# Residual rows of a projection loaded ahead, and its turns moved to the end of the next block

## The chip, the cores and the metric

One core of a Trainium2 chip runs the whole program. The metric is device time in microseconds (us) of one execution, the median of three runs. Profiles show one execution each; times in a profile count from the start of its span. The engines are PE (TensorE: matrix products), PEld (its weight loads), DVE (VectorE), ACT (ScalarE), POOL (GpSimd) and SP (SyncE, which issues the transfers).

## What is computed

The kernel is one layer of a decoder for 512 prompt rows and 32 sample rows (8 sequences of 4), width 1024. Three parts follow each other, each between two RMS norms and added to the residual:

```python
x = x + rms_norm(mix @ w_out, g_mix_post)
x = x + rms_norm(mem_attend(rms_norm(x, g_mem_pre), mk, mv, w_mq, w_mo), g_mem_post)
f, conv_new = conv_ffn(rms_norm(x, g_ffn_pre), conv_buf, w_up, w_dw, b_dw, w_down)
x = x + rms_norm(f, g_ffn_post)
```

The first is a mixer (mLSTM heads and differential attention), the second attends to 256 memory tokens and ends in the output projection `w_mo`, the third is a gated MLP of width 2752 with a causal convolution of three rows. The change lies at the end of the second: `o @ w_mo`, its norm, the sum with the residual, and the turn of the new rows for the products with `w_up`.

## The kernel before, in words

**Blocks.** The 544 rows are five blocks: 0 to 3 are prompt rows of 128, block 4 the 32 sample rows. Rows with the model width in the free dimension are what norms and sums need; products with `w_up` need them turned (width in the partitions). The turned rows are `fT`, in four tiles (a high and a low part for each half of the width, since every product of 32-bit numbers is made as three products of rounded parts: high x high, high x low, low x high).

**The projection.** `proj_add` (L1067) builds two passes over the five blocks, one for each half (512 columns) of `w_mo`. Pass 1 (`ev0`) leaves each block's first half, times the gain, in `y0`, and its sum of squares. Pass 2 (`second`, L1125) is the block-major branch of `gemmA` (L391 to L404): blocks in the order 4, 0, 1, 2, 3, and in each block eight steps k of three products (L387, L388, L389; for block 4 the sample's products at L367). Ahead of a block, `before(b)` (L1088) takes a tile `xb` from the pool N and issues the load of the block's residual rows from DRAM (L1091). After a block, `ev1` (L1093) does on ACT the square sum (L1076), on DVE the multiplication by the gain (L1100) and the sum of the square sums (L1101), on POOL the reciprocal root (`rstd`, L293 and L294), on DVE two operations `STT` (L1106: y times the root plus the residual rows, into `xb`), and on SP the store of the new rows (L1107). Then `rows_of` (L1112) puts the block on the list `pend` and takes on ACT the sum of squares of the new rows into a tile `hN` of the same pool N (L299), which becomes `rsd` (L1118).

**The turns.** `norm_turn` (L311) turns a block on `pend`: two times four transposes on PE (L318) into a PSUM tile `tp`, one multiplication by the next gain on DVE (L320, `ht`), a cast on ACT (L142) and a subtraction on POOL (L143), which write high and low part of `fT`. `mid` (L1121) is called at step `MIDK` = 4 of each block of pass 2 and turns one block if more than `LP` = 1 are pending. So block 4 is turned in the middle of block 1, block 0 in block 2, block 1 in block 3, and blocks 2 and 3 are still pending at the end.

**What follows.** `gemmB` with `half_first` (L433) makes the first four column tiles of `w_up`: first the columns 0 to 255 (blocks 0 and 1) of all four (L439, 128x256), then the columns 256 to 543 (blocks 2, 3 and 4; 128x288). After the first and the third tile (`POS` = (0, 2), L1612) a pending block is turned. The norm of the rows is applied afterwards: `spread` (L1529) makes `rsb`, the roots of all rows spread over the partitions, with a product for each block (L1533). The other tiles of `w_up` and the products with `w_down` go on to the end (L451, L1658 to L1660).

**Weights.** A list of weight tiles is loaded ahead into 6 staging tiles (`wst`; L227 for `w_mo`, L247 for `w_up`) and split on ACT and DVE (L142, L143) into 4 slots (`wslot`). The sample's products read the staging tile itself, so it stays in use until they are done.

**Pools.** N has 5 tiles of 1032 columns (`xb`, `hN`, and before them the queries and the conv rows `cr`); S has 11 large tiles (8.5 KB in each partition: `oT`, `fT`, the conv table `cvT`, keys and values of the memory, later `yp` and `act`). All loads are issued by SP, in one queue.

**Order.** A planner of the language's library sets the order of every engine's instructions from a simulated time line, with the written order as priority; waits are made by it too.

Of the kernel before, what the change touches and what calls it, by code (L numbers as in the profile page):

```python
# [7 lines left out]
F32 = mybir.dt.float32  # L8
# [7 lines left out]
P = 128  # L16
DM = 1024
# [56 lines left out]
def kernel(ctx: ExitStack, tc: tile.TileContext, I, O):  # L74
# [7 lines left out]
    MIDK, LR, LP, POS = 4, 0, 1, (0, 2)  # L82
# [15 lines left out]
    def S(shape, dt, name):  # L98
        return sp.tile(list(shape), dt, name=name, tag="S")

    def N(name, w=1024):
        return npool.tile([P, 1032], F32, name=name, tag="N")[:, :w]

    def T2(shape, name, dt=F32):
        return t2p.tile(list(shape), dt, name=name, tag="T2")

    def Z(name):
        return zp.tile([P, 512], F32, name=name, tag="Z")
# [4 lines left out]
    def mmp(name="mm"):  # L113
        return psm.tile([P, 512], F32, name=name, tag="mm")
# [20 lines left out]
    dma = nc.sync.dma_start  # L135
# [9 lines left out]
    def rows(b):  # L145
        return (b * P, P) if b < 4 else (SEQ, NS)
# [58 lines left out]
    def stage():  # L205
        return stg.tile([P, 1024], F32, name="wst", tag="st")
# [84 lines left out]
    def rstd(ss, n, w, dim, name="rs"):  # L291
        r = small(w, name)
        nc.gpsimd.tensor_scalar(out=r[:n], in0=ss, scalar1=1.0 / dim, scalar2=EPS, op0=MUL, op1=ADD)  # L293
        GTT(out=r[:n], in0=r[:n], in1=mhalf[:n, :w], op=ALU.pow)  # L294
        return r[:n]

    def sumsq(x, n, junk, name="ssq"):
        ss = small(1, name)
        ACT(out=junk, in_=x, func=AF.Square, accum_out=ss[:n])  # L299
        return ss[:n]  # L300
# [29 lines left out]
    class Fill:  # L330
# [8 lines left out]
        def run(self, amount=1e9):  # L339
            while amount > 0 and self.q:  # L340
                try:
                    amount -= next(self.q[0])
                except StopIteration:
                    self.q.pop(0)
# [15 lines left out]
    def sample_mm(ps, xs, w, start, stop):  # L360


        for kk, x in enumerate(xs):
            n = x.shape[0]
            for e in range(2):
                g = NS * (2 * kk + e)
                mm(ps[g:g + NS, :256], lhsT=x, rhs=w[:n, kk, 256 * e:256 * e + 256], start=start, stop=stop)  # L367

    def sample_sum(ps, dst):
        for e in range(2):  # L370
            c = slice(256 * e, 256 * e + 256)
            nc.scalar.copy(out=dst[:, c], in_=ps[NS * e:NS * e + NS, :256])
            VTT(out=dst[:, c], in0=ps[64 + NS * e:64 + NS * e + NS, :256], in1=dst[:, c], op=ADD)

    def gemmA(xt, nk, blocks, evac, block_major=False, before=None, mid=None):


        ps = {}

        def one(b, k, s):  # L380
            if b == 4:
                if k % 2 == 0:
                    sample_mm(ps[b], [xt.sam(k), xt.sam(k + 1)], s[1], k == 0, k == nk - 2)
                return
            s, kk = s[0], k % 2
            c0, n = rows(b)
            mm(ps[b], lhsT=xt.hi(k, c0, c0 + n), rhs=s[:, 0, kk, :], start=(k == 0), stop=False)  # L387
            mm(ps[b], lhsT=xt.hi(k, c0, c0 + n), rhs=s[:, 1, kk, :], start=False, stop=False)  # L388
            mm(ps[b], lhsT=xt.lo(k, c0, c0 + n), rhs=s[:, 0, kk, :], start=False, stop=(k == nk - 1))  # L389

        if block_major:  # L391
            slots = [W.get() for _ in range((nk + 1) // 2)]
            for b in blocks:
                if before:
                    before(b)
                ps[b] = mmp()
                for k in range(nk):
                    if k == MIDK and mid:
                        mid()
                    one(b, k, slots[k // 2])  # L400
                    if b == blocks[-1] and k % 2 == 1:
                        W.free()
                evac(b, ps[b])
                yield 5.1  # L404
        else:
            for b in blocks:
                ps[b] = mmp()
            behind = []
            for k in range(nk):
                if k % 2 == 0:  # L410
                    s = W.get()
                    if 4 in blocks:
                        behind.append((k, s))
                for b in blocks:
                    if b < 4:
                        one(b, k, s)
                if k % 2 == 1:
                    W.free()
                yield sum(0.64 for b in blocks if b < 4)
            for b in blocks:  # L420
                if b < 4:
                    evac(b, ps[b])
            if behind:
                for k, s in behind:
                    one(4, k, s)
                evac(4, ps[4])
                yield 4 * 0.53
            yield 0
# [199 lines left out]
    for c0, c1 in HALF:  # L628
# [5 lines left out]
        t = T2([64, n], "gt")  # L634
# [250 lines left out]
    for g in range(2):  # L885
        for h in range(0, H, 2):
            t = stage().rearrange("p (j b e) -> p j b e", j=2, b=4)
# [174 lines left out]
    def gbc(name):  # L1062
        g = cst.tile([P, 1028], F32, name="gb", tag="gb")
        dma(out=g[:, :DM], in_=I[name][0].partition_broadcast(P))
        return g[:, :DM]

    def proj_add(xt, gname, src, gname2, dst, order=None, scale=None):  # L1067

        g = gbc(gname)
        y0, s0, xb, pend, ready, target = {}, {}, {}, [], [], []  # L1070

        def ssq(b, y, nm):
            n = rows(b)[1]
            ss = sm.tile([P, 1], F32, name=nm, tag=nm, bufs=6)
            j = Z("sqj")
            ACT(out=j[:n], in_=y, func=AF.Square, accum_out=ss[:n])  # L1076
            return ss[:n]

        def ev0(b, ps):
            n = rows(b)[1]  # L1080
            z = y0[b] = T2([P, 512], "y0")[:n]
            if b == 4:
                sample_sum(ps, z)
                ps = z
            s0[b] = ssq(b, ps, "ssy0")
            VTT(out=z, in0=ps, in1=g[:n, :512], op=MUL)

        def before(b):  # L1088
            n = rows(b)[1]
            xb[b] = N("xb")[:n]  # L1090
            dma(out=xb[b], in_=src(b))  # L1091

        def ev1(b, ps):  # L1093
            c0, n = rows(b)
            z = T2([P, 512], "y1")[:n]
            if b == 4:
                sample_sum(ps, z)
                ps = z
            ss = ssq(b, ps, "ssy1")
            VTT(out=z, in0=ps, in1=g[:n, 512:], op=MUL)  # L1100
            VTT(out=ss, in0=s0[b], in1=ss, op=ADD)  # L1101
            rs = rstd(ss, n, 1, DM)
            x = xb[b]
            for i, z in enumerate((y0[b], z)):
                c = slice(512 * i, 512 * i + 512)
                STT(out=x[:, c], in0=z, scalar=rs, in1=x[:, c], op0=MUL, op1=ADD)  # L1106
            dma(out=dst[c0:c0 + n, :], in_=x)  # L1107
            ready.append((x, n, c0))
            while len(ready) > LR:
                rows_of(*ready.pop(0))  # L1110

        def rows_of(x, n, c0):  # L1112
            if scale is None:
                pend.append((norm_rows(x, n, ACTROWS), n, gname2, target[0], c0, POOLQ))
                return
            pend.append((x, n, gname2, target[0], c0, POOLQ))
            rs = sm.tile([P, 1], F32, name="rsd", tag="rsd", bufs=5)
            VCP(out=rs[:n], in_=rstd(sumsq(x, n, N("hN")[:n]), n, 1, DM))  # L1118
            scale[1].append((rs[:n], c0, n))

        def mid():  # L1121
            if len(pend) > LP:
                norm_turn(*pend.pop(0))

        def second(xt2):  # L1125
            target.append(xt2)
            run(gemmA(xt, 8, [4, 0, 1, 2, 3], ev1, block_major=True, before=before, mid=mid))
            while ready:
                rows_of(*ready.pop(0))
            while len(pend) > 2:  # L1130
                norm_turn(*pend.pop(0))
            return pend
        return gemmA(xt, 8, order or allb, ev0, block_major=order is not None), second
# [157 lines left out]
    pend = second(hqT)  # L1291
# [138 lines left out]
    for b in range(4):  # L1430
        t = mk_scores(b)
    with tc.issue_after(t):
        for j in range(8, 16):
            t = mk_turn(j)
# [7 lines left out]
    with tc.issue_after(t):  # L1442
        for b in range(4, NB):
            t = mk_scores(b)
# [81 lines left out]
    rsb = cst.tile([P, ROWS], F32, name="rsb")  # L1526
    rss = []

    def spread(i):  # L1529
        while rss and (i or len(rss) > 2):  # L1530
# [3 lines left out]
            VCP(out=rsb[:, c0:c0 + n], in_=ps[:, :n])  # L1534

    proj, second = proj_add(oT, "g_mem_post", lambda b: xd[0][rows(b)[0]:rows(b)[0] + rows(b)[1], :], "g_ffn_pre", xd[1],
                            scale=(rsb, rss))
    run(proj)
    pend = second(fT)

# [100 lines left out]
    for gi, js in enumerate(groups):  # L1641
# [6 lines left out]
        nk = len(js)  # L1648
# [41 lines left out]
        if not last:  # L1690
            behind = []
            for n0 in (0, 512):
                ps = [mmp() for _ in range(4)]
                for i in range(nk):
# [3 lines left out]
                    for b in range(4):  # L1698
                        t = one(b, ps[b], i, s)
# [124 lines left out]
```

## Time and profile before

| | us |
|---|---|
| median of 3 runs (lowest, highest) | 970.07 (969.19, 971.19) |
| the profiled execution's own time | 968.01 |
| its span, first to last instruction | 966.2 |
| PE busy in the span | 940.1 (97%) |
| DVE, ACT, POOL busy | 598.6, 388.0, 202.6 |
| mean granted clock | 0.989 of 2.4 GHz |

The span is what the engines took; 1.8 us lie around it. A busy PE is not a PE at its peak, since matrix products overlap each other; what counts is where it waits and which clock it is granted. The projection's pass 2 and the start of `w_up` lie at 520 to 583 us of the span.

### The profile page before, as it was taken

Reading aid. Unit: us, or ns where it says so; the run is one execution under the profiler, and the core shown is the slowest. Engines: PE = TensorE matmul, PEld = TensorE weight load, DVE = VectorE, ACT = ScalarE, POOL = GpSimd, SP = SyncE. Lnnn points to the kernel's source line nnn. Section 1 sums busy time; section 2 is a strip of 40 time slices with the busy share of each in tenths; the row PEclk is TensorE's granted clock in tenths of the full one; section 3 lists DMA queues with packets and bytes.
Section 4 is the critical chain, followed back from the end, with each engine's and each line's share of the span. In section 5 each row is a group of like instructions: output and inputs, shape, how many; then the busy total and the mean of one; then the engine's idle time right before and its main releaser. Section 6 shows DMA issues by size and latency. Waiting matters only on the chain.

```text
span 966.2 us, 17070 instructions
## 1 busy us (share of the span) xinstructions
PE 940.1 (97%) x6615; PEld 813.3 (84%) x6615; DVE 598.6 (62%) x1127; ACT 388.0 (40%) x746; POOL 202.6 (21%) x397
## 2 busy tenths in 40 slices
PE   8999999999999999999999799999999999999994
PEld 5999787779866788998767699989988997997983
DVE  6835145555786367625554759827758675675677
ACT  6744134343686367534533524332212222222232
POOL 6610000016332124200000544301110110110114
PEclk9999999999999999999999999999999999999997
DMA  9950024344835359846734844063053303503213
GB/s 303 299 160 1 1 88 134 88 126 133 256 100 173 133 180 322 258 144 209 287 133 128 229 138 128 4 174 89 5 142 79 120 25 91 150 25 90 86 48 114
DMA packets 120529, 130.27 MB, mean 135 GB/s; under 512 B 8551, under 2 KB 85960, under 8 KB 120448
## 3 DMA queue, kind: packets, MB, share of 16 engines
q1 hardware_dynamic: 114264, 125.69, 41.9%
q10 hardware_dynamic: 6184, 3.48, 1.2%
q8 instruction: 52, 0.85, 0.4%
q14 instruction: 29, 0.24, 0.1%
HBM read 112.22 MB, written 16.93 MB: 134 GB/s over the span
## 4 chain that ended last, share of the span: by engine, by line
PE 86%; DVE 4%; DMA 4%; ACT 2%; POOL 2%; issue 1%; SPq 0%; DVEq 0%; POOLq 0%; ACTq 0%
PE mm L451 32%; PE mm L439 8%; PE mm L387 6%; PE mm L389 6%; PE mm L388 6%; PE mm L1660 4%; PE mm L1659 4%; PE mm L1658 4%; PE mm L367 2%; PE tpk L1388 1%; PE sda L1183 1%; DMA xb<-in_x_prompt_dram 1%; DMA wst<-in_w_mo_dram 1%; PE sca L1339 1%; DVE wslot L143 1%
## 5 line engine op out<-in xcount | busy, mean ns | idle before, releaser
L451 PEld LDWEIGHTS mm<-fT,wslot 128*128 128x128 f32 x1872 | 234.3, 188 | 2.1 <-issue 1.2
L451 PE MATMUL mm<-fT,wslot 128*128 128x256 f32 (+1 forms) x1872 | 236.0, 288 | 0.0
L142 ACT CAST wslot<-wst 128x1024 fp32r<-128x1024 f32 x125 | 131.1, 1051 | 254.7 <-PE mm L451 76.0
L143 DVE TENSOR_TENSOR wslot<-wst,wslot 128x1024 fp32r<-128x1024 f32 x125 | 155.7, 1249 | 90.9 <-ACT wslot L142 90.9
L1659 PE MATMUL mm<-wslot,act 128*128 128x512 f32 x176 | 69.6, 396 | 0.0
L1660 PE MATMUL mm<-wslot,act 128*128 128x512 f32 x176 | 68.9, 397 | 0.0
L1658 PE MATMUL mm<-wslot,act 128*128 128x512 f32 x176 | 68.7, 392 | 0.0
L1565 POOL COPY cvo<-u 128x2 f32<-128x2 f32 x43 | 15.2, 354 | 201.2 <-DVE u L1563 191.2
L387 PE MATMUL mm<-wslot,hT 128*128 128x512 f32 x128 | 52.2, 408 | 0.0
L388 PE MATMUL mm<-wslot,hT 128*128 128x512 f32 x128 | 51.3, 401 | 0.0
L389 PE MATMUL mm<-wslot,hT 128*128 128x512 f32 x128 | 51.3, 402 | 0.0
L1560 DVE TENSOR_TENSOR u<-mm,rsb 128x256 f32<-128x256 f32 x43 | 18.2, 424 | 52.9 <-PE mm L451 50.9
L451 PE MATMUL mm<-hT,wslot 128*128 128x256 f32 (+1 forms) x384 | 51.0, 289 | 0.0
L451 PEld LDWEIGHTS mm<-hT,wslot 128*128 128x128 f32 x384 | 49.2, 188 | 0.8 <-issue 0.4
L1658 PEld LDWEIGHTS mm<-wslot,act 128*128 128x128 f32 x176 | 33.6, 191 | 8.6 <-issue 0.8
L1659 PEld LDWEIGHTS mm<-wslot,act 128*128 128x128 f32 x176 | 33.1, 188 | 7.2
L1660 PEld LDWEIGHTS mm<-wslot,act 128*128 128x128 f32 x176 | 33.1, 188 | 7.2
L1577 ACT ACTIVATE c<-c 128x560 f32<-128x560 f32 x21 | 14.1, 672 | 54.9 <-DVE c L1571 51.6
L1571 DVE SCALAR_TENSOR_TENSOR c<-u,cvT,c 128x560 f32<-128x560 f32 x43 | 34.2, 796 | 0.8
L1570 DVE SCALAR_TENSOR_TENSOR c<-u,cvT,c 128x560 f32<-128x560 f32 x43 | 34.1, 792 | 0.1
L439 PE MATMUL mm<-fT,wslot 128*128 128x256 f32 (+1 forms) x192 | 27.2, 303 | 2.6 <-POOL fT L143 2.4
L1671 DVE TENSOR_TENSOR yp<-mm,yp 128x512 f32<-128x512 f32 x40 | 27.1, 687 | 3.9 <-PE mm L1660 3.8
(469 smaller groups left out, 1868.3 us busy)
## 6 DMA issues: line engine op xcount, KB each, us to landing
wst<-in_w_up_dram SPq DMA_DIRECT2D x42, 512.0 KB
wst<-in_w_in_dram SPq DMA_DIRECT2D x28, 512.0 KB
wst<-in_w_down_dram SPq DMA_DIRECT2D x20, 512.0 KB
wst<-in_cache_mem_k_dram SPq DMA_DIRECT2D x16, 512.0 KB
wst<-in_w_mk_dram SPq DMA_DIRECT2D x8, 512.0 KB
xb<-in_x_prompt_dram SPq DMA_DIRECT2D x8, 512.0 KB
wst<-in_cache_dk_dram SPq DMA_DIRECT2D x16, 256.0 KB
wst<-in_cache_dv_dram SPq DMA_DIRECT2D x16, 256.0 KB
```

Source lines behind the costliest of these rows:

```text
L142: nc.scalar.copy(out=hi, in_=src)
L143: (eng or nc.vector).tensor_tensor(out=lo, in0=src, in1=f32(hi), op=SUB)
L387: mm(ps[b], lhsT=xt.hi(k, c0, c0 + n), rhs=s[:, 0, kk, :], start=(k == 0), stop=False)
L388: mm(ps[b], lhsT=xt.hi(k, c0, c0 + n), rhs=s[:, 1, kk, :], start=False, stop=False)
L389: mm(ps[b], lhsT=xt.lo(k, c0, c0 + n), rhs=s[:, 0, kk, :], start=False, stop=(k == nk - 1))
L439: mm(ps, lhsT=s[:, l, k, :], rhs=x(k, c0, c1), start=(k == 0 and j == 0), stop=(k == 7 and j == 2))
L451: mm(ps[i], lhsT=s[:, l, k, :], rhs=x(k, c0, c1), start=(k == 0 and j == 0), stop=(k == 7 and j == 2))
L1570: STT(out=c, in0=u[:, 1:EXT - 1], scalar=w[1], in1=c, op0=MUL, op1=ADD)
L1571: STT(out=c, in0=u[:, 0:EXT - 2], scalar=w[0], in1=c, op0=MUL, op1=ADD)
L1658: mm(ps, lhsT=t[:, 0, c0:c0 + P], rhs=s[:, 0, i % 2, :], start=st, stop=False)
L1659: mm(ps, lhsT=t[:, 0, c0:c0 + P], rhs=s[:, 1, i % 2, :], start=False, stop=False)
L1660: return mm(ps, lhsT=t[:, 1, c0:c0 + P], rhs=s[:, 0, i % 2, :], start=False, stop=en)
```

## The change

Residual rows: with `early=True` the loads of blocks 0 to 3 are issued at the start of `proj_add`, into two tiles of the pool S (two blocks in each); `before` then loads block 4 alone. Turns: `mid` is called at step 7, the last of a block, and turns as soon as one block is pending. So block 4 is turned at the end of block 0, block 0 at the end of block 1, and so on, and block 3 alone is left for the start of `w_up`. Only the memory's projection is called so; the mixer's keeps the old arguments.

```diff
-    def gemmA(xt, nk, blocks, evac, block_major=False, before=None, mid=None):
+    def gemmA(xt, nk, blocks, evac, block_major=False, before=None, mid=None, midk=4):
...
-                    if k == MIDK and mid:
+                    if k == midk and mid:
                         mid()
...
-    def proj_add(xt, gname, src, gname2, dst, order=None, scale=None):
+    def proj_add(xt, gname, src, gname2, dst, order=None, scale=None, early=False):
+
 
         g = gbc(gname)
         y0, s0, xb, pend, ready, target = {}, {}, {}, [], [], []
+        midk, lp = (7, 0) if early else (MIDK, LP)
+        if early:
+            for b in range(4):
+                if b % 2 == 0:
+                    t = S([P, 2, DM], F32, "xb2")
+                xb[b] = t[:, b % 2]
+                dma(out=xb[b], in_=src(b))
...
         def before(b):
+            if b in xb:
+                return
             n = rows(b)[1]
             xb[b] = N("xb")[:n]
             dma(out=xb[b], in_=src(b))
...
         def mid():
-            if len(pend) > LP:
+            if len(pend) > lp:
                 norm_turn(*pend.pop(0))
...
-            run(gemmA(xt, 8, [4, 0, 1, 2, 3], ev1, block_major=True, before=before, mid=mid))
+            run(gemmA(xt, 8, [4, 0, 1, 2, 3], ev1, block_major=True, before=before, mid=mid, midk=midk))
...
     proj, second = proj_add(oT, "g_mem_post", lambda b: xd[0][rows(b)[0]:rows(b)[0] + rows(b)[1], :], "g_ffn_pre", xd[1],
-                            scale=(rsb, rss))
+                            scale=(rsb, rss), early=True)
```

## Rows read from the trace of the kernel before

**Rows 1.** The page, part 1: busy us of each engine.
```profile
PE 940.1 (97%) x6615; PEld 813.3 (84%) x6615; DVE 598.6 (62%) x1127; ACT 388.0 (40%) x746; POOL 202.6 (21%) x397
```

**Rows 2.** Waits of PE, 515 to 585 us: us in total, times, longest.
```profile
PE mm L439 <- POOL fT L143: 2.4, 1, 2.4
PE rsb L1533 <- DVE ht L320: 2.3, 1, 2.3
```

**Rows 3.** Windows: length, busy us by engine (instructions), granted clock, DMA share, GB/s.
```profile
495.00:520.00 25.00, 25.00 (x117) 19.61 (x119) 8.27 (x21) 6.13 (x14) 0.00 (x0) 1.00 0.02 9
...
548.00:556.00 8.00, 3.08 (x19) 2.32 (x17) 8.00 (x12) 3.89 (x8) 7.48 (x10) 0.79 1.08 309
552.60:559.40 6.80, 4.38 (x22) 4.08 (x21) 5.55 (x7) 1.15 (x2) 4.86 (x5) 0.50 1.10 325
545.00:557.70 12.70, 7.78 (x41) 6.45 (x40) 12.70 (x18) 6.83 (x11) 9.98 (x10) 0.80 0.93 264
572.00:900.00 328.00, 328.00 (x2326) 303.91 (x2325) 224.57 (x384) 88.89 (x105) 47.11 (x169) 1.00 0.31 89
```

**Rows 4.** The chain that ended last, 490 to 600 us: start, us, what.
```profile
541.59 0.23 PE mm L388
...
555.57 6.01 PE mm L439 x34
561.58 0.87 PE tp L318 x8
562.46 4.15 PE mm L439 x35
...
567.48 2.73 PE mm L439 x23
570.21 0.45 PE rsb L1533 x4
570.65 12.87 PE mm L439 x96
```

**Rows 5.** Time line of SP's queue: start, us (a group's first to last), operation.
```profile
491.07 29.85 SPq L227 DMA_DIRECT2D wst<-in_w_mo_dram  x4
521.02 9.58 SPq L247 DMA_DIRECT2D wst<-in_w_up_dram  x6
534.65 0.33 SPq L1107 DMA_DIRECT2D x_d<-xb  x1
535.03 0.42 SPq L1091 DMA_DIRECT2D xb<-x_d  x1
...
540.89 0.43 SPq L1091 DMA_DIRECT2D xb<-x_d  x1
...
558.21 0.38 SPq L1091 DMA_DIRECT2D xb<-x_d  x1
```

**Rows 6.** Time line of DVE: the residual additions of blocks 4, 0, 1, 2.
```profile
533.22 1.40 DVE L1106 SCALAR_TENSOR_TENSOR xb<-y,rs,xb 32x512 f32<-32x512 f32 x2
...
539.08 1.41 DVE L1106 SCALAR_TENSOR_TENSOR xb<-y,rs,xb 128x512 f32<-128x512 f32 x2 [1.92 <-DMA xb<-x_d]
...
545.82 1.40 DVE L1106 SCALAR_TENSOR_TENSOR xb<-y,rs,xb 128x512 f32<-128x512 f32 x2
...
554.24 3.52 DVE L1106 SCALAR_TENSOR_TENSOR xb<-y,rs,xb 128x512 f32<-128x512 f32 x2
```

**Rows 7.** Time line of ACT: square sums of blocks 4 and 0 in pass 2.
```profile
530.28 0.63 ACT L1076 ACTIVATE sqj<-y 32x512 f32<-32x512 f32 x1 [0.49 <-DVE y L373]
...
531.83 0.60 ACT L1076 ACTIVATE sqj<-mm 128x512 f32<-128x512 f32 x1 [0.82 <-PE mm L389]
```

**Rows 8.** Time line of PE: the turns of blocks 0 and 1.
```profile
543.52 1.04 PE L318 MATMUL tp<-cpk,xb 128*128 128x128 f32 x8
...
547.64 1.03 PE L318 MATMUL tp<-cpk,xb 128*128 128x128 f32 x8
```

**Rows 9.** L143 on POOL, 515 to 575 us: duration ns min/median/max, first and last start.
```profile
L143 POOL TENSOR_TENSOR fT<-ht,fT x10: 457/1296/2280, 542.8 to 570.9; 128x512 fp32r<-128x512 f32 x8, 128x128 fp32r<-128x128 f32 x2
```

## The prediction

> **What bounds the kernel now.** I read the page first: TensorE is busy for 97% of the span [rows 1], so only time in which it stands still, or runs at half its clock, can be won by a change of order like this one. Then the waits of TensorE around the memory's output projection: two of them are long, 2.4 us on GpSimd writing fT (the turned rows that feed w_up) and 2.3 us on VectorE emptying a turn's PSUM tile [rows 2]. The table by windows gives their weight: between 548 and 556 us TensorE works 3.08 of 8 us, while VectorE is busy all 8.00 and GpSimd 7.48; in 552.6 to 559.4 the granted clock is 0.50, the 1.2 GHz level, against 1.00 on either side [rows 3]. The fall comes after the gaps, and it shows in the chain: 34 products of w_up's first half take 6.01 us from 555.57, the next 35 only 4.15 us [rows 4].
>
> Why is fT late? The queue of SP tells it. Each load of a block's residual rows (xb) stands right behind the store of the block before it: 534.65 store, 535.03 load; the next load is at 540.89, the last at 558.21 [rows 5]. A store waits for VectorE's two residual additions (L1106), so a block's load cannot leave before the block ahead is finished. The additions of the sample block (4) and of blocks 0, 1 and 2 start at 533.22, 539.08, 545.82 and 554.24 [rows 6], while a block's 24 products take only 24 x 0.23 = 5.5 us [rows 4]. The rows fall further behind the products with each block; block 1, which w_up's first half needs, is turned at 547.64, after the last product of block 3 [rows 8].
>
> **Cost of the change, part by part.** What matters is the stretch from the end of block 1's turn (about 548.5) to the start of w_up's second half at 570.65 [rows 4]: 22.15 us. The work in it: 96 products at 4.15/35 = 0.1186 us, 11.39 us; two turns of 0.87 us, 1.74; four groups of rsb products, bounded by 0.45 us each, 1.8 [rows 4]. Sum 14.9, so **7.2 us are lost**. Counted the other way: idle 8.00 - 3.08 = 4.92 us [rows 3], and the half clock 6.01 - 34 x 0.1186 = 1.98 us, 6.9 together. I take 7.2 as all that can be won here.
>
> Loads ahead. Four loads of 512 KB leave L1091 and come before the projection, into two of the 11 large buffers, where they no longer wait for a slot of the small pool or for a store. Their place in SP's queue is after the first writes of the conv table (cvT takes its large buffer before them), about 495 us. There SP holds the last two w_mo loads until 520 (a group of four issues that spans 29.85 us) [rows 5], and the DMA engines move 9 GB/s from 495 to 520 [rows 3]. 2.1 MB at the 309 GB/s of the busy window 548 to 556 [rows 3] are 6.8 us, inside these 25 us of quiet. Four issues of 0.4 us cost SP nothing then. If the cover is gone (they stand behind the held w_mo loads), they meet w_mo and six w_up loads from 520 on and cost up to 6.8 us of DMA time; that is a rival. Buffers: four for oT, one for cvT and two for these loads leave four, which is what fT needs; the tiles of the next stage come when oT is done. I take no cost; a late buffer would delay fT, whose bound is in the next step.
>
> Turns. Each is eight transposes, two multiplications on VectorE, two casts and two subtractions, as many as before. Block 1's moves from the middle of block 3 (step 4) to the end of block 2 (step 7): five steps of 3 x 0.23, 3.45 us earlier; block 2's moves ahead of w_up, 0.87 us that TensorE pays earlier and not twice; only block 3's is left beside w_up's first half. When can a block's rows be ready? The sample block, whose residual rows had long been loaded, shows the chain alone: square sum at 530.28 [rows 7], additions done at 533.22 + 1.40 = 534.62 [rows 6], 4.34 us. Block 0's products end at 531.8 [rows 7]. Block 1's end is worked out backwards: block 3 ends at about 547.4, takes 5.5 and a turn of 0.9, and block 2 5.5 and the sample's turn, so block 1 ends near 535. Its rows are then ready at 539.3, against 547.2 now, and the end of block 2 (541) is late enough for its turn.
>
> From turn to fT: now 547.64 to 555.57, 7.9 us with VectorE and GpSimd full [rows 4, 8]. The floor is 0.87 for the transposes, 0.7 for a multiplication, 0.6 for a cast and 2 x 1.30 for GpSimd's median subtractions [rows 9], 4.8 us. So fT of block 1 is there between 541 + 4.8 = 545.8 and (547.64 - 3.45) + 7.9 = 552.1. TensorE, with block 2's turn paid earlier, can begin w_up at 547.4 + 0.9 + 0.45 = 548.8. The wait that remains lies between 0 and 3.3 us; I take 1.0, nearer the floor, since the turn falls into a stretch before VectorE's full one (545 to 557.7: 12.70 of 12.70 [rows 3]).
>
> Second half: block 3's rows are ready at 547.4 + 4.3 = 551.7, and even with the slow 7.9 us fT is there at 559.6. W_up's first half ends at 548.8 + 1.0 + 11.4 + 0.9 = 562.1. Covered. Afterwards TensorE is busy for 328.00 of 328.00 us [rows 3], so a shift there should carry to the end.
>
> **Sum:** 7.2 - 1.0 = 6.2 us off the profiled execution's 968.01, 961.8. The median of the runs shown is 970.07, 2.06 us more, so I predict 963.9. A measurement of this kernel tells about 0.2%, 1.9 us, from no change.
>
> **Rivals.**
> Loads late. If SP's order puts the four loads behind the held w_mo loads and the six of w_up, they land between 531 and 542 instead of by 503. Against it: cvT is written long before 520. The chain of stores is gone even then, but blocks 0 and 1 come some 2 to 3 us later than above: gain about 3.5, 966.6.
>
> The congestion moves. For it: VectorE and GpSimd are both full where fT is made, and a pair of residual additions that takes 1.40 us at 545.82 takes 3.52 at 554.24 [rows 6], beside GpSimd's subtractions, which run from 1296 ns at the median to 2280 [rows 9]. If each addition waits out a whole subtraction, fT comes at the late bound, 552.1: 3.3 us of wait, gain 3.9, and 1 to 2 us of it back to a lower clock: 967.6. Against it: the same work is spread over more time. The Trainium skill (SBUF — State Buffer, section "SBUF: two separate sides") calls VectorE's and GpSimd's common port pair an exclusive lock, where the loser blocks for the whole instruction. The trace agrees in kind (1.40 against 3.52 us), and by that rule this rival is the likelier wherever turns overlap additions.
>
> Nothing won. The order of each engine's instructions is set by a planner over the whole program: step 7 is a priority, not a place (block 1's turn is written into the middle of block 3 now and runs after its end). If it puts the turns where they are today, the gap stays: 970.1.
>
> Slower. TensorE takes its queue in order, and a turn now stands ahead of a block's last products. If it is held at its written place, TensorE waits for rows: for the sample's 3.5 us (step 7 of block 0 at 531.1, rows at 534.62) and for block 0's 2.1 us (rows at 531.8 + 4.34 = 536.1, step 7 of block 1 at about 534, since part of block 1 runs before block 0 ends). Half a clock for 6.8 us, as after the gaps now, costs 3.4 more [rows 3]; if additions take 3.52 instead of 1.40 us, blocks 1 and 2 stop it for 1.5 each. Sum 12.0 against 7.2: 974.9. It decides when rows come more than one block of products, 5.5 us, after a block's end. Against it: today no turn makes TensorE wait [rows 2]; the sample's is put off into block 2.
>
> **Chances.** The forecast 0.62 (its own range 961.3 to 966.5); loads late 0.12; congestion 0.10; nothing won 0.08; slower 0.08. The low end is 970.07 - 7.2 - 1.6 for a run at the bottom of the spread and a small gain from the planner's new order, 961.3; the high end takes in the first three rivals, 970.1. Faster by over 0.2% is the first three cases less a little, 0.83; within 0.2% 0.09; slower 0.08.
>
> **What would show it.** Right: the four loads issued between 491 and 505; all four turns but block 3's before the last product; no wait of TensorE on fT over 1.5 us; granted clock 1.00 through 545 to 572; w_up's second half begins near 564. A step is wrong if loads leave after 520 (loads late), if fT's wait stays with loads early (congestion), or if transposes wait for xb (slower). If the second half begins at 564 and the end does not move by as much, the claim that TensorE carries the shift is wrong.

## The result, and the profile after

Before 969.72 us, after 972.43 us (medians of 22 runs each; 967.49 to 972.86 and 969.34 to 976.30). The ratio is **1.0026 [1.0018, 1.0034]**: slower by 0.26%, about 2.5 us. The prediction, 963.9 us and "faster" with a chance of 0.83, was wrong, and the result lies above its whole range, 961.3 to 970.1.

The profiled execution of after took 972.98 us with a span of 971.2, 5.0 longer than before's. Not all of that can be put down to the change. The first of the sample's products in pass 2 starts at 522.97 in after and at 519.34 in before, with the same products in the same order ahead of it; by the 200th instruction of TensorE, far ahead of the changed code, the two are already 4.3 us apart (47.25 and 42.97). In the 14 profiled executions of this study that first product lies anywhere from 518.26 to 523.78. So I count from it. **The stretch** below runs from there to the first product of L451, which closes the first four column tiles of `w_up`; from its end to the end of the program every one of these executions takes 382.9 us.

The stretch in before, a row by windows (length, then busy us of PE, PEld, DVE, ACT and POOL with instructions, granted clock, DMA share, GB/s):

```profile
519.34:583.36 64.02, 59.10 (x403) 51.00 (x403) 41.46 (x74) 25.84 (x49) 26.35 (x44) 0.95 0.68 201
```

The same view of after: the stretch, then the windows that answer to [rows 3] and one where the clock fell.

```profile
522.97:588.30 65.33, 59.12 (x403) 50.88 (x403) 44.40 (x76) 27.75 (x51) 24.85 (x44) 0.95 0.56 166
495.00:520.00 25.00, 24.27 (x113) 19.47 (x111) 10.08 (x24) 6.03 (x12) 0.00 (x0) 1.00 0.36 126
548.00:556.00 8.00, 4.51 (x25) 3.39 (x24) 8.00 (x8) 5.45 (x9) 3.16 (x3) 1.00 0.45 119
556.20:563.00 6.80, 4.28 (x18) 3.98 (x19) 5.72 (x8) 2.29 (x4) 5.08 (x5) 0.50 0.87 249
575.60:903.60 328.00, 328.00 (x2326) 303.92 (x2325) 224.64 (x386) 88.59 (x105) 40.42 (x168) 1.00 0.31 89
```

The stretch grew by 1.31 us. TensorE is busy for as long as before, 59.1 us; all of the 1.31 is idle time, 6.21 against 4.92. The clock falls to the 1.2 GHz level as before, for 6.8 us. Between 495 and 520 the transfers moved 126 GB/s instead of 9: these are the loads, ahead of time as predicted. SP's queue shows them (start, us, operation, number), the answer to [rows 5]:

```profile
494.75 1.31 SPq L227 DMA_DIRECT2D wst<-in_w_mo_dram  x2
496.12 2.24 SPq L1078 DMA_DIRECT2D xb<-x_d  x4
523.67 0.90 SPq L227 DMA_DIRECT2D wst<-in_w_mo_dram  x2
```

What TensorE waited for between 518 and 590 us (us in total, times, longest), the answer to [rows 2]:

```profile
PE tp L318 <- DVE xb L1116: 2.9, 1, 2.9
PE mm L439 <- ACT fT L142: 1.7, 1, 1.7
PE mm L439 <- POOL fT L143: 1.6, 1, 1.6
```

Busy times of the engines (the page's part 1, [rows 1]) and the subtractions on POOL (count, ns min/median/max, first and last start, [rows 9]) changed by at most 7 us, so no engine became the bound:

```profile
PE 942.0 (97%) x6615; PEld 814.4 (84%) x6615; DVE 599.6 (62%) x1127; ACT 387.9 (40%) x746; POOL 195.9 (20%) x397
```

```profile
L143 POOL TENSOR_TENSOR fT<-ht,fT x10: 462/1292/2119, 543.2 to 573.0; 128x512 fp32r<-128x512 f32 x8, 128x128 fp32r<-128x128 f32 x2
```

The first of the three waits is new: a turn (L318) waits for the residual additions (now L1116). TensorE's time line shows which turn, the answer to [rows 8] (in brackets the idle time before it and what ended that):

```profile
545.07 0.60 PE L318 MATMUL tp<-cpk,xb 128*128 128x128 f32 x4
...
548.76 0.60 PE L318 MATMUL tp<-cpk,xb 128*128 128x128 f32 x4
...
551.29 0.60 PE L318 MATMUL tp<-cpk,xb 128*128 128x128 f32 x4
554.80 0.63 PE L318 MATMUL tp<-cpk,xb 128*128 128x128 f32 x4 [2.92 <-DVE xb L1116]
557.10 1.01 PE L439 MATMUL mm<-fT,wslot 128*128 128x256 f32 x3 [1.67 <-ACT fT L142]
559.73 4.32 PE L439 MATMUL mm<-fT,wslot 128*128 128x256 f32 x22 [1.63 <-POOL fT L143]
```

These are the turns of block 0 (545.07, 548.76) and block 1 (551.29, 554.80). Each has come apart into its two halves, 3.7 and 3.5 us from one to the next, where before all eight transposes ran together [rows 8]. The first half of block 1's turn comes 28.3 us into the stretch, and so it did before (547.64 - 519.34). The loads left some 40 us earlier, and block 1 is turned no sooner. VectorE's time line tells why its rows are late, the answer to [rows 6]:

```profile
536.19 0.16 DVE L1111 TENSOR_TENSOR ssy<-ssy,ssy 128x1 f32<-128x1 f32 x1 [0.76 <-ACT sqj L1084]
...
539.55 0.16 DVE L1111 TENSOR_TENSOR ssy<-ssy,ssy 128x1 f32<-128x1 f32 x1 [1.79 <-ACT sqj L1084]
...
540.67 0.75 DVE L1116 SCALAR_TENSOR_TENSOR xb<-y,rs,xb 128x512 f32<-128x512 f32 x1 [0.37 <-POOL rs L294]
542.49 0.54 DVE L320 TENSOR_TENSOR ht<-tp,gT 128x128 f32<-128x128 f32 x2 [1.07 <-PE tp L318]
542.95 0.68 DVE L1110 TENSOR_TENSOR y<-mm,gb 128x512 f32<-128x512 f32 x1
...
544.09 0.74 DVE L1116 SCALAR_TENSOR_TENSOR xb<-y,rs,xb 128x512 f32<-128x512 f32 x1
...
547.74 1.78 DVE L1116 SCALAR_TENSOR_TENSOR xb<-y,rs,xb 128x512 f32<-128x512 f32 x1 [0.36 <-POOL rs L294]
...
550.58 0.68 DVE L320 TENSOR_TENSOR ht<-tp,gT 128x512 f32<-128x512 f32 x1
551.18 0.68 DVE L1110 TENSOR_TENSOR y<-mm,gb 128x512 f32<-128x512 f32 x1
...
552.91 1.75 DVE L1116 SCALAR_TENSOR_TENSOR xb<-y,rs,xb 128x512 f32<-128x512 f32 x1
```

In the order of the rows: sums of squares of blocks 0 and 1, then block 0's addition in two halves (540.67, 544.09), then block 1's (547.74, 552.91). Two holds can be read here. The sum of squares of block 0 is there at 536.35 and that of block 1 at 539.71 (the two L1111 rows), but the first halves of their additions start at 540.67 and 547.74, each released by the root on POOL. And the second halves, 544.09 and 552.91, come some 3 and 5 us behind the first, each behind a multiplication L1110 (y of the second half) that stands behind a turn's L320. POOL's time line shows the first hold:

```profile
535.78 0.54 POOL L294 TENSOR_TENSOR rs<-rs,mhalf 32x1 f32<-32x1 f32 x1
539.03 0.18 POOL L293 TENSOR_SCALAR rs<-ssq 32x1 f32<-32x1 f32 x1 [2.71 <-ACT hN L299]
539.29 0.19 POOL L293 TENSOR_SCALAR rs<-ssy 128x1 f32<-128x1 f32 x1
...
546.09 0.19 POOL L293 TENSOR_SCALAR rs<-ssq 128x1 f32<-128x1 f32 x1 [2.01 <-ACT hN L299]
546.36 0.19 POOL L293 TENSOR_SCALAR rs<-ssy 128x1 f32<-128x1 f32 x1
...
547.68 1.29 POOL L143 TENSOR_TENSOR fT<-ht,fT 128x512 fp32r<-128x512 f32 x1
...
551.99 2.12 POOL L143 TENSOR_TENSOR fT<-ht,fT 128x512 fp32r<-128x512 f32 x1 [3.02 <-ACT fT L142]
```

There are two roots for each block. `rs<-ssy` is the one that its additions need; `rs<-ssq` is that of its finished rows, which nothing needs before `rsb`. The second root of block 4 stands ahead of the first root of block 0. It waits 2.71 us for ACT's square sum over the sample's finished rows, and block 0's root, whose input was ready at 536.35, waits behind it until 539.29. Block 1's waits from 539.71 to 546.36 behind the second root of block 0. The Trainium skill (Perfetto Trace Analysis, section "Tensor Engine Instruction (MATMUL, LD_WEIGHTS)") calls ACT, VectorE and GpSimd strict FIFO; these rows agree.

**Theory.** The rows are late because of two orders: (1) a block's root waits on POOL behind the previous block's second root, as it did in before; (2) y of the second half takes a tile of the pool T2, which also holds the turns' `ht`. With `LP` = 0 the turn of block b-1 is written ahead of block b's `ev1`, so y of b stands behind that turn, and so does the second half of its addition. **Rivals:** the place of the turns itself costs (a turn at the head of TensorE's queue holds up the products behind it); or the load chain was the whole loss, and the new buffers cost something elsewhere.

### The profile page after: what moved, and what is told of

Read it like the earlier page. It is cut to its first block, busy times and chain, and to the rows that moved or that the text cites. A ratio compares the mean times of both kernels' runs of the same rounds, so it can differ in the third digit from the quotient of the medians.

```text
span 971.2 us, 17068 instructions
## 1 busy us (share of the span) xinstructions
PE 942.0 (97%) x6615; PEld 814.4 (84%) x6615; DVE 599.6 (62%) x1127; ACT 387.9 (40%) x746; POOL 195.9 (20%) x397
## 4 chain that ended last, share of the span: by engine, by line
PE 86%; DMA 5%; DVE 4%; ACT 2%; issue 2%; POOL 1%; SPq 0%; DVEq 0%; POOLq 0%; ACTq 0%
PE mm L451 31%; PE mm L439 8%; PE mm L387 6%; PE mm L389 6%; PE mm L388 6%; PE mm L1670 4%; PE mm L1669 4%; PE mm L1668 4%; PE mm L367 2%; DMA xb<-in_x_prompt_dram 1%; PE sda L1193 1%; PE tpk L1398 1%; DMA wst<-in_w_mo_dram 1%; PE sca L1349 1%; PE cpo L1379 1%
## 5 line engine op out<-in xcount | busy, mean ns | idle before, releaser
L451 PEld LDWEIGHTS mm<-fT,wslot 128*128 128x128 f32 x1872 | 234.3, 188 | 2.1 <-issue 1.2
L451 PE MATMUL mm<-fT,wslot 128*128 128x256 f32 x1872 | 236.0, 288 | 0.0
L143 DVE TENSOR_TENSOR wslot<-wst,wslot 128x1024 fp32r<-128x1024 f32 x125 | 155.2, 1244 | 89.3 <-ACT wslot L142 89.3
L1575 POOL COPY cvo<-u 128x2 f32<-128x2 f32 x43 | 11.0, 257 | 210.2 <-DVE u L1573 200.2
L451 PE MATMUL mm<-hT,wslot 128*128 128x256 f32 (+1 forms) x384 | 51.0, 289 | 0.0
L451 PEld LDWEIGHTS mm<-hT,wslot 128*128 128x128 f32 x384 | 49.2, 188 | 0.8 <-issue 0.4
L1580 DVE SCALAR_TENSOR_TENSOR c<-u,cvT,c 128x560 f32<-128x560 f32 x43 | 34.1, 792 | 0.1
L439 PE MATMUL mm<-fT,wslot 128*128 128x256 f32 (+1 forms) x192 | 28.3, 305 | 3.3 <-ACT fT L142 1.7
L439 PEld LDWEIGHTS mm<-fT,wslot 128*128 128x128 f32 x192 | 26.5, 202 | 3.9 <-POOL fT L143 1.9
```

Source lines behind the costliest of these rows:

```text
L143: (eng or nc.vector).tensor_tensor(out=lo, in0=src, in1=f32(hi), op=SUB)
L439: mm(ps, lhsT=s[:, l, k, :], rhs=x(k, c0, c1), start=(k == 0 and j == 0), stop=(k == 7 and j == 2))
L451: mm(ps[i], lhsT=s[:, l, k, :], rhs=x(k, c0, c1), start=(k == 0 and j == 0), stop=(k == 7 and j == 2))
L1580: STT(out=c, in0=u[:, 1:EXT - 1], scalar=w[1], in1=c, op0=MUL, op1=ADD)
```

## The experiments

In the table, rows of block 1 are ready when the second half of its addition ends; half clock is the time at the 1.2 GHz level inside the stretch; times are of one profiled execution each, from the start of the stretch. Ratios are against the kernel before, on the same chip, from 5 to 12 runs of each experiment.

| run | loads ahead | turns moved | y in PSUM | roots moved | ratio [95%] | stretch | PE idle | half clock | rows of block 1 |
|---|---|---|---|---|---|---|---|---|---|
| before | | | | | | 64.0 | 4.9 | 6.8 | 27.9 |
| after | x | x | | | 1.0026 [1.0018, 1.0034] | 65.3 | 6.2 | 6.8 | 31.7 |
| e1_loads_only | x | | | | 0.9984 [0.9973, 0.9996] | 63.1 | 3.3 | 6.8 | 24.9 |
| e2_turns_only | | x | | | 1.0041 [1.0025, 1.0058] | 67.9 | 6.8 | 10.2 | 34.1 |
| e3_in_psum | x | x | x | | 1.0023 [1.0009, 1.0036] | 65.8 | 5.1 | 10.2 | 25.5 |
| e4_psum_root | x | x | x | x | 0.9964 [0.9951, 0.9977] | 59.1 | 2.1 | none | 20.2 |
| e5_root_only | x | x | | x | 0.9987 [0.9970, 1.0005] | 62.4 | 4.2 | 3.4 | 32.9 |
| e6_loads_psum_root | x | | x | x | 0.9940 [0.9926, 0.9954] | 58.9 | 1.9 | none | 20.2 |
| e7_turns_psum_root | | x | x | x | 0.9969 [0.9953, 0.9985] | 62.6 | 2.8 | 6.8 | 21.1 |
| e8_loads_psum | x | | x | | 1.0006 [0.9991, 1.0020] | 65.4 | 4.9 | 10.2 | 25.5 |
| e9_loads_root | x | | | x | 0.9947 [0.9935, 0.9960] | 58.2 | 1.0 | none | 23.2 |
| e10_root_old | | | | x | 0.9935 [0.9916, 0.9954] | 57.8 | 0.9 | none | 22.9 |

### The change in two halves

Loads ahead, turns where they were:

```diff
-        midk, lp = (7, 0) if early else (MIDK, LP)
+        midk, lp = MIDK, LP
```

> The loads ahead alone; turns at step 4 with one block left pending, as before. The stretch from the sample's products of pass 2 to the first product of w_up's third tile is 64.0 us in the kernel before and 65.3 in the changed one, and 7.2 us of the 64.0 were idle or at half clock. Tile order (a turn written ahead of the next block's second multiplication holds up that block's rows, since both take tiles from one pool in written order): the loads are good and the turns are bad, stretch 60 to 62, 2 to 4 us faster than before. Root order (GpSimd takes the root for the sum of squares of a block's new rows ahead of the next block's own root, and so waits for the additions of the block before): that chain stays, stretch 63 to 64, no change. Place (a turn at step 7 makes TensorE wait, nothing else is wrong): stretch 57 to 60, 4 us faster or more.

Turns at the new place, each load in its old place:

```diff
-        if early:
-            for b in range(4):
-                if b % 2 == 0:
-                    t = S([P, 2, DM], F32, "xb2")
-                xb[b] = t[:, b % 2]
-                dma(out=xb[b], in_=src(b))
```

> The turns' new place alone; residual rows loaded as before, one block at a time. Tile order: as slow as the changed kernel or slower, stretch 65 to 67, 2 to 4 us slower than before, with the same pairs of a split residual addition. Root order: loads and roots both hold the rows, 65. If the loads ahead were what harms (their two large buffers, or the traffic), this one would be faster than before.

Measured: 0.9984 and 1.0041. The loads win about 1.6 us, the turns lose about 4. The stretch of e1_loads_only, 63.1, lies where the root order put it (63 to 64), not where the tile order did (60 to 62): with the turns written as before, a hold is left. TensorE's waits in e1_loads_only, and then in e2_turns_only:

```profile
PE rsb L1543 <- DVE ht L320: 3.3, 1, 3.3
```

```profile
PE tp L318 <- DVE xb L1110: 4.6, 1, 4.6
PE mm L439 <- POOL fT L143: 0.8, 1, 0.8
```

With the old turns no turn waits. With the new ones TensorE stands at block 1's turn, 2.9 us in after and 4.6 without the early loads. So the two halves pull against each other, and the loss is tied to the moved turns. Whether the place of the turns costs by itself, or only what else they put in order, is the next question.

### The two holds

The tile: y of blocks 0 to 3 is written over its own product in PSUM and takes no tile of T2. The written order stays.

```diff
-            z = T2([P, 512], "y1")[:n]
+            z = ps if early and b < 4 else T2([P, 512], "y1")[:n]
```

> The changed kernel, with the second multiplication of blocks 0 to 3 written back into its PSUM tile, so that it takes no tile of the pool that the turns use. Tile order: the two halves of each residual addition come together again, rows of block 1 ready 4 us earlier than in the changed kernel, stretch 59 to 62, 2 to 5 us faster than before. Root order: little, 63 to 65. Place: as the changed kernel, 65, since the turns stand where they stood.

The roots (`lastroot` holds the last root that was queued): `rows_of` only notes the block; its square sum, second root and `rsd` are written after the next block's evacuation and queued behind that block's own root (and the last at the end of pass 2). This on top of e3_in_psum:

```diff
...
+            root = lastroot[0]
...
+            if early:
+                while stats:
+                    with tc.issue_after(root.ins):
+                        stat(*stats.pop(0))
...
+        def stat(x, n, c0):
+            rs = sm.tile([P, 1], F32, name="rsd", tag="rsd", bufs=5)
+            VCP(out=rs[:n], in_=rstd(sumsq(x, n, N("hN")[:n]), n, 1, DM))
+            scale[1].append((rs[:n], c0, n))
...
-            rs = sm.tile([P, 1], F32, name="rsd", tag="rsd", bufs=5)
-            VCP(out=rs[:n], in_=rstd(sumsq(x, n, N("hN")[:n]), n, 1, DM))
-            scale[1].append((rs[:n], c0, n))
+            stats.append((x, n, c0))
...
```

> The one before, and besides the sum of squares of a block's new rows is taken after the next block's evacuation, with its root queued on GpSimd behind that block's own root. Tile order: like the one before within 1 us. Root order: another 2 to 4 us, stretch 57 to 59, 5 to 7 us faster than before. Place: 65.

Measured: 1.0023 and 0.9964. VectorE in e3_in_psum, blocks 0 and 1:

```profile
538.19 0.75 DVE L1116 SCALAR_TENSOR_TENSOR xb<-y,rs,xb 128x512 f32<-128x512 f32 x1 [0.30 <-POOL rs L294]
538.86 0.75 DVE L1116 SCALAR_TENSOR_TENSOR xb<-mm,rs,xb 128x512 f32<-128x512 f32 x1
...
544.13 0.75 DVE L1116 SCALAR_TENSOR_TENSOR xb<-y,rs,xb 128x512 f32<-128x512 f32 x1
544.80 0.75 DVE L1116 SCALAR_TENSOR_TENSOR xb<-mm,rs,xb 128x512 f32<-128x512 f32 x1
```

Without the tile the two halves come together again and block 1's rows are 6.2 us earlier (25.5 against 31.7). The second hold was thus the tile, since the edit touches nothing else of the order. But the time did not move, against the 59 to 62 us of stretch expected from the tile: TensorE now stands 2.6 us at block 2's turn (the profile names no releaser; the turn's first half goes as soon as the first half of that block's addition ends, 31.9 into the stretch), and the clock stays down for 10.2 us instead of 6.8. POOL in this run has the second root of block 1 ahead of block 2's own:

```profile
546.94 1.05 POOL L293 TENSOR_SCALAR rs<-ssq 128x1 f32<-128x1 f32 x1
548.07 0.19 POOL L293 TENSOR_SCALAR rs<-ssy 128x1 f32<-128x1 f32 x1
```

With the roots moved as well (e4_psum_root), the stretch is 59.1, 6.3 us shorter than after's, and of TensorE's waits this is left:

```profile
PE mm L441 <- POOL fT L143: 1.7, 1, 1.7
PE rsb L1557 <- DVE ht L322: 0.4, 1, 0.4
```

### One mend at a time, each with the turns in either place

Four combinations of the edits above: e5_root_only is after with the roots moved alone; the other three are named after what they hold.

> The changed kernel with the moved square sums and roots alone; the second multiplication takes its tile from the turns' pool again. If both holds count (tile order and root order), this is between the changed kernel (stretch 65.3) and the one with both mended (59.1): 61 to 63.5, with a residual addition still split, near the kernel before or 2 us faster. If the root order were all, it would be as fast as with both: 59, 966.8 us. If the tile order were all, 65.

> Both mended, and the turns written at step 4 with one pending, so that block 2's turn comes after w_up has begun. If block 2's turn ahead of w_up costs something by itself (TensorE standing at it), this is 1 to 2 us faster than with both mended and the change's place: stretch 57 to 58. If that cost is gone as soon as the rows come in time, the two are equal within 1 us: 58.5 to 60.

> Both mended, the turns at the change's place, but the residual rows loaded one block at a time as before. If the loads ahead are worth what the plain comparison says (the kernel with loads ahead alone is 1 to 2 us faster than before; the one with the turns alone 2.5 us slower in its stretch than with both), this is 2 to 4 us slower than with the loads ahead: stretch 61 to 63. If the load of a block only followed the other two holds, it is as fast: 59 to 60.

> Loads ahead, the second multiplication in PSUM, turns at step 4 with one pending. It differs from the third experiment (stretch 65.8) only in where the turns are written. Place: TensorE no longer stands 3.2 us at block 2's turn, and the clock falls for a shorter time, stretch 61.5 to 63.5, 2 to 3 us faster than the third. If the place were not to blame there, 65 to 66.

Measured: 0.9987, 0.9940, 0.9969 and 1.0006.

- e5_root_only: the roots alone win 2.9 us of the stretch at the new place, and TensorE stands 4.2 us at the second half of block 1's turn, waiting for the addition. There the tile still holds: the first half of block 1's addition ends 18.6 into the stretch, the second only at 32.9, against 20.2 with both mends.
- e6_loads_psum_root against e4_psum_root: only the place of the turns differs, and with both holds gone the stretch is 58.9 against 59.1. In the profiles the new place costs nothing by itself, and it gains nothing either: block 1 is turned 25.7 into the stretch in both. Between the runs, 0.9940 and 0.9964 are 2.3 us apart with intervals that just overlap, so a cost of that size is not excluded.
- e7_turns_psum_root against e4_psum_root: the early loads make block 1's rows 0.9 us earlier (in e7_turns_psum_root block 0's load leaves early too, for the reason given under e10_root_old below, so this is what the other loads are worth). The stretch differs by 3.5, since in e7_turns_psum_root the clock fell and in e4_psum_root it did not; the runs, 0.9969 and 0.9964, show no difference that can be told.
- e8_loads_psum against e1_loads_only: y in PSUM at the old place of the turns. The stretch is 2.3 us longer, with a longer fall of the clock. This mend is not free, and at the old place it has little to mend. Against e3_in_psum only the place differs, 65.4 and 65.8: with the roots in the old order the new place costs little by itself either.

### Again, and the roots without the rest

The kernels before and after once more, unchanged, with the roots moved on top of e1_loads_only, and the roots moved in the kernel before.

> The kernel before once more, for the same reason: same waits, stretch 63.5 to 64.5, no difference from its other runs beyond 0.1%.

> The changed kernel once more. Its first profile is 1.3 us slower in the stretch and to the end, its runs 2.5 us slower than before. If the rest lies in what differs from one execution to the next (the clock's first rise at the start, the length of its fall after the gaps), a second profile shows the same waits and another start or fall; stretch 65 to 67.

> Loads ahead and the roots moved, turns at step 4 with one pending, and the second multiplication in the turns' pool as before. There it is written ahead of the turn of the block before, not behind it. Tile order: that pool is harmless at the old place, so this is as good as the versions with both mended, stretch 58.5 to 60.5, 4 to 5 us faster than before, against 62.4 for the same mend at the change's place. If the pool held up the rows at either place, 62 to 63.

> The kernel before with the roots moved alone: no load ahead, turns at the old place. If the root order was what held the rows in the kernel before, and not the loads, stretch 60 to 63 and 2 to 4 us faster than before, with nothing of the change in it. If the loads held them, as the prediction had it, 63.5 to 64.5 and no change.

Measured: r_before 1.0000 [0.9986, 1.0015], r_after 1.0020 [1.0006, 1.0035], with stretches of 63.8 and 65.6, so the loss repeats. e9_loads_root 0.9947; e10_root_old **0.9935** [0.9916, 0.9954], 963.41 us against 970.32. That edit alone, with nothing of the change in it, beats both kernels, before by about as much as the change was predicted to, and by more than the 2 to 4 us expected of it. POOL in e10_root_old:

```profile
532.69 0.62 POOL L295 TENSOR_SCALAR rs<-ssy 128x1 f32<-128x1 f32 x1 [0.70 <-DVE ssy L1107]
...
535.18 0.64 POOL L295 TENSOR_SCALAR rs<-ssq 32x1 f32<-32x1 f32 x1 [0.85 <-ACT hN L301]
...
536.53 0.19 POOL L295 TENSOR_SCALAR rs<-ssy 128x1 f32<-128x1 f32 x1
...
537.43 0.19 POOL L295 TENSOR_SCALAR rs<-ssq 128x1 f32<-128x1 f32 x1
```

The order is turned round: each block's own root (ssy) now runs ahead of the second root (ssq) of the block before it. TensorE's waits in this kernel, and then its clock by windows:

```profile
PE mm L441 <- POOL fT L143: 0.9, 1, 0.9
```

```profile
546.00:560.00 14.00, 13.13 (x100) 12.15 (x99) 12.35 (x20) 7.17 (x12) 11.52 (x16) 1.00 0.81 242
```

One wait of 0.9 us is left and the clock stays at the 2.4 GHz level, 1.00. Adding the early loads to this (e9_loads_root) brings nothing more. Block 1 is turned 25.5 into the stretch here, with the turns at the old place. One caution: the edit does more than turn POOL's order. It also takes `hN` of block 4 from the pool N behind `xb` of block 0, and so block 0's load leaves early. SP's queue in e10_root_old:

```profile
466.33 0.33 SPq L1097 DMA_DIRECT2D xb<-x_d  x1
534.32 0.42 SPq L1097 DMA_DIRECT2D xb<-x_d  x1
```

The load at 466.33 is block 0's, which in before left at 535.03 [rows 5]; the next is block 1's. Block 0's load can thus leave without the store that the prediction took for its condition. So in e10_root_old the share of POOL's order and that of the freed load are not told apart. With all loads ahead, e1_loads_only against e9_loads_root shows the order without the load: 63.1 to 58.2, 4.9 us of the stretch. (The edit moves the second square sums on ACT together with the roots; it is POOL's rows that show the wait.)

## Why the prediction was wrong

**The loads: right in place, small in worth.** They left at 496.12, forecast "about 495"; the transfers had room; none of TensorE's waits in the stretch was for a buffer. They won 1.6 us by themselves; the 6.2 was forecast for loads and turns together.

**The step that failed: "when can a block's rows be ready".** It took 4.34 us from a block's products to its rows from the sample block, called this "the chain alone", and put block 1's rows at 539.3. The end of block 1's products it had right: near 535 in before's time, 15.7 into the stretch; after shows the sum of squares 16.6 to 16.7 into it. But the rows came at 31.7, about 16 us after the products. The size of the bare chain was not the error: with both holds gone (e4_psum_root, e6_loads_psum_root) block 1's rows come 20.2 into the stretch, where 539.3 lies at 20.0. What the step put at nothing are the two holds: with both in place, in after, the rows come 11.5 us later. The sample block is first in its pass: no block's second root stands ahead of its own on POOL, and no turn ahead of its y in T2. It showed a chain without a predecessor and was used for blocks that have one. The hold on POOL was there to be read, in the trace of before:

```profile
535.89 0.18 POOL L293 TENSOR_SCALAR rs<-ssq 32x1 f32<-32x1 f32 x1 [3.20 <-ACT hN L299]
536.15 0.19 POOL L293 TENSOR_SCALAR rs<-ssy 128x1 f32<-128x1 f32 x1
```

The second root of block 4 runs ahead of the first root of block 0, after a wait on ACT. But there block 0's load landed later still (the 1.92 us that VectorE waits for the transfer in [rows 6]), so the waits named the transfer. Removing the last of two waits showed the one beneath it.

**The turns: wrong in time and in cost.** Forecast: block 1's turn 3.45 us earlier. Measured: not earlier at all, and its second half waits 2.92 us in TensorE's queue. Once the rows come in time (e4_psum_root) block 1 is turned 25.7 into the stretch instead of 28.3, 2.6 us earlier; but so it is at the old place (25.7 in e6_loads_psum_root, 25.5 in e10_root_old). Rows in time were enough for that, and no run shows a gain from the new place. What I did not count is that moving a turn in the written order also moves its tiles ahead of another step's tiles of the same pool.

**What could be won: right in size.** "7.2 us are lost": e10_root_old gets back 6.2 of the stretch, e9_loads_root 5.8, with the full clock, though by another edit than the one predicted. Both halves of that loss were seen rightly, the gap and the half clock after it. That a shift carries to the end was right too: 382.9 us follow the stretch in every kernel.

**The rivals.** "Loads late" and "nothing won" did not happen. "Congestion" came in part: two waits for fT, 3.3 us together, as much as the bound that the forecast gave, but by another course: they follow the late turn and shrink to 1.7 when it comes in time. "Slower" (0.08) had the right place and mechanism: a turn at the head of TensorE's queue, waiting for rows. Its condition, rows later than 5.5 us after a block's end, was met. Its sum, 12.0 against 7.2, was wrong in both terms: TensorE did not wait at the turns of the sample and of block 0, and the 7.2 to set against them were not won. Its chance should have been larger, since the case against it rested on the 4.34 us.

**What stays open.** The runs say +2.5 and +1.9 us (after, r_after), the stretches +1.3 and +1.8. The 1.8 lies within its interval (0.6 to 3.4 us), the 1.3 below its own (1.7 to 3.3); so about 1 us (2.5 - 1.3) may lie ahead of the stretch, where both profiles of the changed kernel run late (522.97 and 523.59, against 519.34 and 518.26). As e6_loads_psum_root, faster than before, starts at 523.78, two profiles of each do not settle it. Nor was it settled why y in PSUM costs 2.3 us in e8_loads_psum.

## What to carry to other kernels

When a wait is to be removed, look for the second-latest input of the same instruction: follow the other operands of the waiting step back through each in-order queue, and ask of each entry there whether anything needs it yet. A duration taken from the first block of a pass holds for the first block alone; the chain of a later block has to be read with the previous block's leftovers in the queues and in the tile pools. When an entry is moved to another place, compare it with the old place after the holds are gone; here the old place did as well. A statistic that is needed late should be queued late: moving the second roots, with all loads ahead, was worth 4.9 us of the stretch, and moving 2 MB of loads alone 0.9.

## What was not expected of the hardware

**The clock falls or holds on little.** In e4_psum_root TensorE is idle for 0.35 and 1.73 us shortly after one another, and the clock stays up; in e7_turns_psum_root for 1.07 and 1.74, and it falls for 6.83 us. First e4_psum_root by windows, then e7_turns_psum_root:

```profile
552.00:562.00 10.00, 9.20 (x78) 9.20 (x79) 5.10 (x11) 2.02 (x4) 8.28 (x12) 1.00 0.70 215
```

```profile
555.20:561.80 6.60, 5.77 (x27) 5.78 (x28) 3.49 (x8) 0.89 (x2) 6.35 (x7) 0.50 0.79 239
```

Of the 3.5 us between their stretches 0.7 is idle time and the rest the slower clock. And where there was one long gap alone, 4.2 us in e5_root_only went with only 3.4 us at the lower level, 3.3 us in e1_loads_only with 6.8. The length of a gap alone does not tell the price.

**One operation, two prices.** A half of the residual addition takes 0.75 us alone (540.67 in after) and 1.78 or 1.75 beside POOL's L143 (547.74 beside 547.68, 552.91 beside 551.99). The Trainium skill (SBUF — State Buffer, section "SBUF: two separate sides") calls the port pair that VectorE and GpSimd share an exclusive lock, held for the whole instruction; these rows agree in kind: the excess is 1.0 us, and when the additions began 1.2 us of POOL's instruction were left (548.97 - 547.74 and 554.11 - 552.91).
